# Gate and up of three feed-forward parts in seven block products instead of eight

## The chip, the cores and the metric

The kernel runs on one core of a Trainium2 chip. The metric is the device time of one execution in microseconds (us); the time given for a kernel is the median of several executions. The profile is one execution, recorded by the hardware. PE is TensorE (matmuls), PEld its weight loads, DVE is VectorE, ACT is ScalarE, POOL is GpSimd, SP issues the DMAs.

## The reference, cut to what matters

One step of an encoder of two layers on 656 tokens (528 of a prompt, 128 new rows of a sample group), width 1024. Each layer is: feed-forward, mixing (state space and latent attention in the first layer, forgetting attention and retention in the second), feed-forward. After each of the six steps comes `x = LN(ALPHA*x + f(x))`. So there are four feed-forward parts, each with 2816 hidden features:

```
hid = silu(x @ w_gate) * (x @ w_up)      # 1024 -> 2816, twice
f   = hid @ w_down                       # 2816 -> 1024
x   = LN(ALPHA * x + 0.5 * f)
```

## The kernel before, in words

Features lie on the partitions, tokens along the columns. The tokens are in two halves, h=0 with 336 and h=1 with 320 columns (320 and 320 from the last feed-forward part on). A feature dimension of 1024 is 8 tiles of 128, the hidden one 22 tiles. Every number is held as a sum of two parts of reduced precision (fp32r), a high one and a low one, so that each product is three matmuls: high by high, high by low, low by high (`mm3`, L286).

The work of a feed-forward part is a list of jobs (`ffn_part`, L406): in four groups of 5, 6, 6 and 5 hidden tiles (`PARTS`) a gate and an up job for each hidden tile, then 8 down jobs. A gate or up job has 8 input tiles: 24 matmuls for each half. A weight tile comes by DMA into a raw slot of the ring, ScalarE writes its high part into a pair slot (`hi`, L274) and VectorE the low part, raw less high (`sub`, L277). ScalarE takes silu of the gate from PSUM (L416); VectorE multiplies by up (L284); ScalarE and VectorE split the result into high and low hidden parts. `dense` (L353) runs each job for h=0, and for h=1 a few jobs later.

At the end of a part each half has its layer norm (`layer_norm`, L508, `scaled`, L541): the mean by two matmuls from column sums (that of h=1 is the "mean" of the second half below), on VectorE the differences and the sum of the squares (ending in the "fold", tile `ffn_lnva`), the variance by one more matmul, a Newton step for the root (tiles `ffn_sg`), products with it into `ffn_lnt`, and from there the next x: high part on ScalarE (L563), x itself on GpSimd (L564, tile `keep_y`), low part on VectorE (L277, tile `keep_x`). While the second half has its layer norm, PE runs the first jobs of what comes next on h=0. Six pair slots let it go six jobs, 144 matmuls, ahead.

The order within each engine is set before the run, by a scheduler with its own estimate of durations; each engine takes its list in that order and waits by semaphores. Where a wait is given by hand (`behind`, the tables `LN_SUBS` and `LN_AFTER`), an instruction is put behind a named step of the layer norm.

## Time and profile before

| | |
|---|---|
| executions | 2788.96, 2790.32, 2798.34 us |
| median | 2790.32 us |
| span of the profiled execution, first to last instruction | 2785.8 us |
| mean granted clock of TensorE | 0.974 |
| PE, DVE, ACT, POOL busy | 2696.4, 1195.6, 851.6, 452.3 us |
| stages of the span | feed-forward 1 to about 480, mixing to 870, feed-forward 2 to 1340, feed-forward 3 to 1840, mixing to 2290, feed-forward 4 to 2764, last layer norm to 2786 |

The table is read from the page, the times and the stretches of the timeline. The span leaves out what lies before the first and after the last instruction. "Granted clock" is the share of TensorE's full 2.4 GHz. Busy time of PE counts a pipelined stream of matmuls as one, so the rate is read as a stretch divided by its number of matmuls.

### The profile page before, as it was taken

To read this page: it belongs to the slowest core of one execution; us is meant where nothing else is said; L and a number is where in the kernel's file an instruction comes from. 1 tells how busy PE (TensorE), PEld (TensorE's weight loads), DVE (VectorE), ACT (ScalarE), POOL (GpSimd) and SP (SyncE) were. 2 spreads that over 40 slices of the span, in tenths; PEclk is the share of its full clock that TensorE was granted. 3 is DMA by queue.
4 is the path that set the end of the run, shared out by engine and by line. 5 is a ranking of instruction groups with operands and counts; after the bars stand their busy time and mean duration, and the time that the engine had idled before them with its cause. 6 is when DMAs were issued, how large, how long until landed. Compare 5 with 4: busy or idle time off the path is not lost.

```text
span 2785.8 us, 42647 instructions
## 1 busy us (share of the span) xinstructions
PE 2696.4 (97%) x17840; PEld 2547.3 (91%) x17840; DVE 1195.6 (43%) x2094; ACT 851.6 (31%) x1509; POOL 452.3 (16%) x569
## 2 busy tenths in 40 slices
PE   9999999899999999999999999989999999999997
PEld 8999999887678999999899999968868889999996
DVE  7343333654347333333733333365332585333335
ACT  3222222435434222222422222243343343222222
POOL 1233311651115000000500000052110041000002
PEclk9999999978999999999999999989999999999998
DMA  4323222342212222222222222112145242222221
GB/s 153 93 90 107 94 92 72 115 123 76 67 50 76 69 80 73 73 80 59 71 68 80 72 71 80 59 55 85 46 159 172 59 140 64 88 67 83 71 70 53
DMA packets 97987, 233.61 MB, mean 84 GB/s; under 512 B 14321, under 2 KB 32898, under 8 KB 97794
## 3 DMA queue, kind: packets, MB, share of 16 engines
q1 hardware_dynamic: 91266, 209.57, 24.6%
q0 software_dynamic: 6528, 21.30, 2.5%
q8 instruction: 140, 2.29, 0.3%
q14 instruction: 53, 0.43, 0.0%
...
## 4 chain that ended last, share of the span: by engine, by line
PE 89%; DVE 5%; POOL 2%; ACT 2%; issue 2%; DMA 1%; DVEq 0%; ACTq 0%; POOLq 0%; SPq 0%
PE psum L255 87%; PE psum L258 2%; POOL keep_y L564 2%; DVE ffn_lnva L284 1%; DVE ffn_sg L284 1%; DVE keep_y L284 1%; DVE ring_pair L277 1%; DVE keep_x L277 1%; DVE ffn_lnt L284 1%; ACT ring_pair L274 0%; DMA ring_raw<-oout 0%; DMA s_w<-d_w 0%; DVE ffn_sg L574 0%; DVE ffn_sg L573 0%; ACT ffn_sg L571 0%
## 5 line engine op out<-in xcount | busy, mean ns | idle before, releaser
L255 PE MATMUL psum<-keep_x,ring_pair 128*128 128x320 f32 (+2 forms) x10608 | 1675.4, 316 | 42.6 <-ACT keep_x L563 13.3
L255 PEld LDWEIGHTS psum<-keep_x,ring_pair 128*128 128x128 f32 (+1 forms) x10608 | 1609.4, 190 | 80.8 <-DVE keep_x L277 24.0
L255 PE MATMUL psum<-ffn_hid,ring_pair 128*128 128x320 f32 (+1 forms) x4224 | 653.8, 312 | 0.0
L255 PEld LDWEIGHTS psum<-ffn_hid,ring_pair 128*128 128x128 f32 x4224 | 635.3, 188 | 1.8 <-issue 0.4
L277 DVE TENSOR_TENSOR ring_pair<-ring_raw,ring_pair 128x1024 fp32r<-128x1024 f32 (+3 forms) x341 | 380.3, 1116 | 554.6 <-ACT ring_pair L274 548.7
L274 ACT ACTIVATE ring_pair<-ring_raw 128x1024 fp32r<-128x1024 f32 (+3 forms) x361 | 343.0, 953 | 868.4 <-PE psum L255 818.3
L284 DVE TENSOR_TENSOR keep_y<-keep_y,psum 128x320 f32<-128x320 f32 (+3 forms) x256 | 139.2, 555 | 282.8 <-PE psum L255 282.5
L284 POOL TENSOR_TENSOR ffn_acc<-keep_y 128x320 f32<-128x320 f32 (+1 forms) x12 | 11.7, 979 | 1390.7 <-DVE keep_y L284 1341.7
L274 ACT ACTIVATE ffn_hid<-ffn_sg 128x320 fp32r<-128x320 f32 (+1 forms) x176 | 83.2, 473 | 321.3 <-DVE ffn_sg L284 321.2
L284 DVE TENSOR_TENSOR ffn_sg<-psum,ffn_sg 128x320 f32<-128x320 f32 (+1 forms) x176 | 87.1, 495 | 214.1 <-PE psum L255 214.0
L416 ACT ACTIVATE ffn_sg<-psum 128x320 f32<-128x320 f32 (+1 forms) x176 | 77.1, 439 | 218.9 <-PE psum L255 218.8
L277 DVE TENSOR_TENSOR ffn_hid<-ffn_sg,ffn_hid 128x320 fp32r<-128x320 f32 (+1 forms) x176 | 101.2, 575 | 66.4 <-ACT ffn_hid L274 66.4
L564 POOL TENSOR_SCALAR keep_y<-ffn_lnt,keep_cst 128x320 f32<-128x320 f32 (+1 forms) x80 | 89.2, 1127 | 65.1 <-DVE ffn_lnt L284 65.1
L284 POOL TENSOR_TENSOR ffn_acc<-ffn_acc,keep_y 128x320 f32<-128x320 f32 (+1 forms) x60 | 62.3, 1039 | 114.9 <-DVE keep_y L284 100.0
L429 DVE SCALAR_TENSOR_TENSOR keep_y<-keep_y,psum 128x336 f32<-128x336 f32 (+1 forms) x64 | 31.6, 494 | 90.0 <-PE psum L255 89.8
L277 DVE TENSOR_TENSOR keep_x<-keep_y,keep_x 128x320 fp32r<-128x320 f32 (+3 forms) x89 | 59.9, 685 | 22.4 <-POOL keep_y L564 16.6
L563 ACT ACTIVATE keep_x<-ffn_lnt,keep_cst 128x320 fp32r<-128x320 f32 (+1 forms) x80 | 47.3, 650 | 51.9 <-DVE ffn_lnt L284 51.9
L916 POOL TENSOR_SCALAR even_prompt_prob<-even_prompt_prob,even_prompt_sm 80x80 f32<-80x80 f32 (+5 forms) x48 | 27.6, 576 | 145.0 <-DVE even_prompt_sm L915 132.5
L255 PE MATMUL psum<-keep_x,even_gate_pair 128*128 128x336 f32 (+1 forms) x288 | 49.6, 321 | 1.1 <-ACT even_prompt_k L1113 0.7
L277 POOL TENSOR_TENSOR ring_pair<-ring_raw,ring_pair 128x1024 fp32r<-128x1024 f32 (+1 forms) x20 | 48.5, 2425 | 5.3 <-PE psum L255 5.2
L255 PEld LDWEIGHTS psum<-keep_x,even_gate_pair 128*128 128x128 f32 x288 | 43.3, 188 | 2.9 <-ACT even_prompt_k L1113 0.9
L913 DVE TENSOR_REDUCE even_prompt_nmx<-psum 80x1 f32<-80x80 f32 (+5 forms) x48 | 25.2, 526 | 33.5 <-PE psum L255 33.2
...
## 6 DMA issues: line engine op xcount, KB each, us to landing
...
```

Source lines behind the costliest of these rows:

```text
L255: return self.nc.tensor.matmul(out, lhsT, rhs, start=start, stop=stop)
L258: self.nc.tensor.transpose(out, in_, ident)
L274: return self.nc.scalar.activation(out, in_, AF.Copy, scale=scale)
L277: return (eng or self.nc.vector).tensor_tensor(out, a, b_r.bitcast(F32), ALU.subtract)
L284: return (eng or self.nc.vector).tensor_tensor(out, a, b, op)
L416: nc.scalar.activation(sg, ps[:, :n], AF.Silu)
L429: nc.vector.scalar_tensor_tensor(y[:, m], y[:, m], 2 * ALPHA, ps[:, :n], ALU.mult, ALU.add)
L563: at["xh", h, m] = nc.scalar.activation(xh[:, m], tm, AF.Identity, scale=g[:, m:m + 1], bias=b[:, m:m + 1])
L564: at["y", h, m] = nc.gpsimd.tensor_scalar(y[:, m], tm, g[:, m:m + 1], b[:, m:m + 1], ALU.mult, ALU.add)
L913: nc.vector.reduce_max(nmx[:rows], sc[:rows, :cols], axis=AX.X, negate=True)
L916: nc.gpsimd.tensor_scalar(p[:rows, :cols], p[:rows, :cols], sm[:rows], 1.0, ALU.mult, ALU.mult)
```

## The change

Gate and up of feed-forward parts 2, 3 and 4 (`bffn`) are computed in blocks. Two hidden tiles (a pair), two halves of the input features (4 tiles each) and two equal halves of the tokens (328 columns, in the last part 320) make a 2 by 2 by 2 product. Before it is 8 block products of 12 matmuls. The change forms sums of weight blocks and sums of x blocks and does with 7 products, P1 to P7, each added into a PSUM bank in a chain: X takes P1, P6, P7, P4, and is copied away between them (`snap`); Y takes P5 and P3; W takes P2.

- Weights: two raw tiles for each pair, gate and up apart. VectorE forms four sums of [128, 512], and each of seven blocks is split into high and low (`bform`) into half a pair slot.
- x: the four sums (`combos`) are formed and split after the second half's layer norm, before each of the three parts. For the input tiles that only sums read (m < 4 of h=1) the layer norm writes x alone, on ScalarE.
- Start of a part: the six gate and up jobs of the first three pairs run their (first hidden tile, first token half) quadrant the ordinary way, 24 matmuls each (`bjob_a`), and load their weights a second time later for the five products that are left.
- The last two products of a job run between the first two of the next one (`run`).
- Groups of hidden tiles are 6, 6, 6, 4 (`SPARTS`). In the last group all eight down jobs run for h=0, then all eight for h=1.
- The ring for these parts has 4 raw and 4 pair slots (8 half slots), before 3 raw and 6 pair slots. The hidden tiles, x sums and tables of the mixing steps share memory anew.

```diff
+    def combos(self):
+        V, w = self.nc.vector, self.wid
+        y = self.Y3
+        b11, b12, b21, b22 = (y[:, 4 * i:4 * i + 4, self.cols(j)] for i in range(2) for j in range(2))
+        at, bt = self.ab("A", F32R), self.ab("B", F32R)
+        def form(tl, c):
+            v = tl[:, 2624 * c:2624 * c + 8 * w].rearrange("p (i k n) -> p i k n", i=2, k=4)
+            return v[:, 0], v[:, 1]
+        xb = lambda i, j: tuple(x[:, 4 * i:4 * i + 4, self.cols(j)] for x in self.X3)
+        f = self.forms_x = dict(P1=xb(0, 0), P2=xb(1, 0), P3=xb(1, 1), P5=xb(0, 1), P6=form(at, 0), P7=form(at, 1), P4=form(bt, 0))
+        for c in (0, 2):
+            s = slice(c, c + 2)
+            def tmp(tag):
+                return self.t(tag, [128, 2, 336], F32, 2, self.lnr)[:, :, :w]
+            def out(p, d):
+                self.split(d, f[p][0][:, s], f[p][1][:, s])
+            d1 = tmp("lnt")
+            self.tt(d1, b11[:, s], b12[:, s], ALU.subtract)
+            d2 = tmp("lnt")
+            V.scalar_tensor_tensor(d2, d1, -1.0, b22[:, s], ALU.mult, ALU.subtract)
+            out("P6", d2)
+            out("P5", d1)
+            d3 = tmp("lnsq")
+            self.tt(d3, b22[:, s], b12[:, s], ALU.subtract)
+            out("P7", d3)
+            d4 = tmp("lnsq")
+            V.scalar_tensor_tensor(d4, d2, -1.0, b21[:, s], ALU.mult, ALU.subtract)
+            out("P4", d4)
+    def bmm(self, ps, f, p, start):
+        xh, xl = self.forms_x[p]
+        for i in range(4):
+            for n, (a, x) in enumerate(((f[:, 0, i], xh[:, i]), (f[:, 0, i], xl[:, i]), (f[:, 1, i], xh[:, i]))):
+                self.nc.tensor.matmul(ps, a, x, start=start and i + n == 0, stop=i == 3 and n == 2, skip_group_check=not start)
+    def bform(self, src):
+        f = self.forms[0]
+        self.forms.rotate(-1)
+        self.split(src, f[:, 0], f[:, 1])
+        return f
...
+    def bconsume(self, gu, q, fi, bank, add, sign):
+        nc = self.nc
+        r, c = q
+        if gu == 0:
+            if q == (0, 0) and add is None:
+                g = self.t("sg", [128, 336], F32, 2, self.fr[0])[:, :self.wid]
+            else:
+                if r == c and (q == (0, 0) or fi not in self.gt):
+                    self.gt[fi] = self.t("lnsq", [128, 2, 336], F32, 2, self.lnr)
+                if q == (1, 0):
+                    self.gt[fi] = self.t("lnsq", [128, 2, 336], F32, 2, self.lnr)
+                g = self.gt[fi][:, c if r == c else r, :self.wid]
+            if add is None:
+                nc.scalar.activation(g, bank, AF.Silu, scale=float(sign))
+            else:
+                self.tt(g, bank, add, ALU.add)
+                nc.scalar.activation(g, g, AF.Silu, scale=float(sign))
+            self.g[fi, q] = g
+            return
+        g = self.g.pop((fi, q))
+        src = bank
+        if add is not None:
+            self.tt(add, bank, add, ALU.add)
+            src = add
+        if sign > 0:
+            self.tt(g, src, g, ALU.mult)
+        else:
+            nc.vector.scalar_tensor_tensor(g, src, -1.0, g, ALU.mult, ALU.mult)
+        hh, hl = (x[:, fi + r, self.cols(c)] for x in self.hidt)
+        self.split(g, hh, hl)
+    def bjob_a(self, ff, p, gu, i):
+        w = self.job_fetch(self.job(self.I["wgu"][ff, 2 * p, gu], None, None), i, LN_AFTER, LN_POOL)
+        ps = self.ps("mm")[:, :self.wid]
+        self.bmm(ps, w[:, :, 0:4], "P1", True)
+        s1 = self.t("s1", [128, 336], F32, 6, self.strr)[:, :self.wid]
+        self.nc.scalar.copy(s1, ps)
+        self.bmm(ps, w[:, :, 4:8], "P2", False)
+        self.pairs.append(w)
+        self.bconsume(gu, (0, 0), 2 * p, ps, None, 1)
+        return s1
+    def bjob(self, ff, p, gu, f0, s1=None):
+        nc, V, w = self.nc, self.nc.vector, self.wid
+        fi = 2 * p - f0
+        raws = []
+        for k in range(2):
+            raw = self.raw[0]
+            self.raw.rotate(-1)
+            self.dma(raw, self.I["wgu"][ff, 2 * p + k, gu])
+            raws.append(raw)
+        a11, a12, a21, a22 = (r[:, 4 * i:4 * i + 4] for r in raws for i in range(2))
+        lead = s1 is not None
+        X = self.ps("mm")[:, :w]
+        def snap(add):
+            u = self.ut[:, len(us), :w]
+            us.append(u)
+            if add is None:
+                nc.scalar.copy(u, X)
+            else:
+                self.tt(u, X, add, ALU.add)
+            return u
+        us = []
+        if not lead:
+            f = self.bform(a11)
+            self.bmm(X, f, "P1", True)
+            s1 = self.t("s1", [128, 336], F32, 6, self.strr)[:, :w]
+            nc.scalar.copy(s1, X)
+            yield
+            f = self.bform(a12)
+            W = self.ps("mm")[:, :w]
+            self.bmm(W, f, "P2", True)
+            self.bconsume(gu, (0, 0), fi, W, s1, 1)
+            yield
+        ut = self.ut = self.t("lnt", [128, 2, 336], F32, 2, self.lnr)
+        s3 = self.t("ws", [128, 4, 128], F32, 2, self.hidr)
+        self.tt(s3, a11, a21, ALU.add)
+        self.tt(a21, a21, a22, ALU.add)
+        self.tt(a11, a21, a11, ALU.add)
+        f = self.bform(a11)
+        self.bmm(X, f, "P6", lead)
+        self.ut = ut
+        u2 = snap(s1 if lead else None)
+        yield
+        f = self.bform(a21)
+        Y = self.ps("mm")[:, :w]
+        self.bmm(Y, f, "P5", True)
+        yield
+        f = self.bform(s3)
+        self.bmm(X, f, "P7", False)
+        self.ut = ut
+        u3 = snap(s1 if lead else None)
+        self.bconsume(gu, (1, 1), fi, Y, u3, -1)
+        yield
+        f = self.bform(a22)
+        self.bmm(X, f, "P4", False)
+        self.bconsume(gu, (1, 0), fi, X, s1 if lead else None, -1)
+        yield
+        self.tt(a12, a11, a12, ALU.add)
+        f = self.bform(a12)
+        self.bmm(Y, f, "P3", False)
+        self.bconsume(gu, (0, 1), fi, Y, u2, 1)
+        yield
+    def bffn(self, ff, ln_idx, last=False, blocks=False):
+        nc = self.nc
+        self.g, self.gt = {}, {}
+        nparts = len(SPARTS)
+        s1 = {}
+        f0, f1 = SPARTS[0]
+        n = 0
+        for p in range(f0 // 2, f1 // 2):
+            for gu in range(2):
+                s1[p, gu] = self.bjob_a(ff, p, gu, n)
+                n += 1
+        self.forms = deque(x[:, :, k:k + 4] for x in self.pairs for k in (0, 4))
+        waiting = None
...
+        def run(job, full):
+            nonlocal waiting
+            steps = 5 if full else 3
+            for i in range(steps):
+                next(job)
+                if i < 2:
+                    advance(waiting)
+            if waiting is not None:
+                assert next(waiting, 0) == 0
+            waiting = job
...
+        ahead = None
+        for pi, (f0, f1) in enumerate(SPARTS):
+            todo = [(p, gu) for p in range(f0 // 2, f1 // 2) for gu in range(2)]
+            for p, gu in todo:
+                if ahead is not None:
+                    ahead = None
+                    continue
+                run(self.bjob(ff, p, gu, f0, s1.get((p, gu))), (p, gu) not in s1)
+            if pi < nparts - 1:
+                p2 = f1 // 2
+                ahead = self.bjob(ff, p2, 0, f1)
+                run(ahead, True)
+                jobs = [down(pi, m) for m in range(8)]
+                for m, j in enumerate(jobs):
+                    wt = self.job_load(j)
+                    for h in range(2):
+                        self.job_run(j, h, wt)
+                        if m == 0:
+                            advance(waiting)
+                    self.pairs.append(wt)
+                assert next(waiting, 0) == 0
+                waiting = None
+        pi = nparts - 1
+        jobs = [down(pi, m) for m in range(8)]
+        halves = deque(x[:, :, k:k + 4] for x in self.pairs for k in (0, 4))
...
+        self.layer_norm(0, ln_idx, 4.0, last, blocks)
+        for m, j in enumerate(jobs):
+            with self.behind(*[("mean", 0, 0)] * (m >= LN_FREE), *[("var", 0, 0)] * (m >= 8 - LN_VAR)):
+                self.job_run(j, 1, w[m])
+        self.layer_norm(1, ln_idx, 4.0, last, blocks)
+        self.pairs = full
...
+            if blocks and h == 1:
+                self.combos()
...
+            elif blocks and m < 4:
+                at["y", h, m] = nc.scalar.activation(y[:, m], tm, AF.Identity, scale=g[:, m:m + 1], bias=b[:, m:m + 1])
...
-        self.ring_more("right", 2, 2)
+        self.ring_more("right", 3, 0)
...
-        self.ring_more("right", 1, 3)
+        self.ring_more("right", 2, 1)
...
-            self.ffn(1, 2)
-            self.ffn(2, 3)
+            self.bffn(1, 2, blocks=True)
+            self.bffn(2, 3)
...
-            self.ffn(3, 5, last=True)
+            self.bffn(3, 5, last=True)
```

Two places in the order of the engines, both at the entry of feed-forward part 3. First PE, before: from the last jobs on the first half (336 columns) past the variance matmul (`ffn_lnva`) of the second half to the first matmuls that read the second half (320 columns).

```order
L255 MATMUL psum<-keep_x_66,ring_pair_6826 128x336 x22
L255 MATMUL psum<-keep_x_66,ring_pair_6827 128x336 x2
L255 MATMUL psum<-ffn_lnva_6841,keep_cst_65 128x320
L255 MATMUL psum<-keep_x_66,ring_pair_6827 128x336 x22
L255 MATMUL psum<-keep_x_66,ring_pair_6828 128x336 x24
L255 MATMUL psum<-keep_x_66,ring_pair_7194 128x320
L255 MATMUL psum<-keep_x_66,ring_pair_7195 128x320
L255 MATMUL psum<-keep_x_66,ring_pair_6825 128x320
L255 MATMUL psum<-keep_x_66,ring_pair_7194 128x320 x3
```

And PE after; `ring_pair` holds weights, `abA` one of the x sums, and `keep_x` with 328 columns is x or the x sum of P5.

```order
L267 MATMUL psum<-ffn_lnva_6844,keep_cst_65 128x320
L549 MATMUL psum<-keep_x_66,ring_pair_6830 128x328
L549 MATMUL psum<-keep_x_66,ring_pair_6831 128x328 x12
L549 MATMUL psum<-keep_x_66,ring_pair_6832 128x328 x12
L549 MATMUL psum<-keep_x_66,ring_pair_6833 128x328 x12
L549 MATMUL psum<-keep_x_66,ring_pair_6832 128x328 x12
L549 MATMUL psum<-keep_x_66,ring_pair_6833 128x328 x12
L549 MATMUL psum<-keep_x_66,ring_pair_6830 128x328
L549 MATMUL psum<-keep_x_66,ring_pair_6832 128x328
L549 MATMUL psum<-keep_x_66,ring_pair_6830 128x328 x5
L549 MATMUL psum<-keep_x_66,ring_pair_6832 128x328 x5
L549 MATMUL psum<-abA_11135,ring_pair_6830 128x328
```

The last row of each is the first that reads the second half. In both, PE has 144 matmuls on the first half before it needs the second; before, the next one reads `keep_x` of h=1 as the layer norm writes it, after, it reads sums formed from it.

Then DVE, before: from the fold of the second half's layer norm on.

```order
L284 TENSOR_TENSOR ffn_lnva_6841<-ffn_lnva_6841 128x320
L277 TENSOR_TENSOR ring_pair_6827<-ring_raw_7193,ring_pair_6827 128x1024
L284 TENSOR_TENSOR ffn_sg_6835<-psum,ffn_sg_6835 128x336
L277 TENSOR_TENSOR ffn_hid_6833<-ffn_sg_6835,ffn_hid_6833 128x336
L284 TENSOR_TENSOR ffn_sg_6834<-psum,ffn_sg_6834 128x336
L277 TENSOR_TENSOR ffn_hid_6833<-ffn_sg_6834,ffn_hid_6833 128x336
L284 TENSOR_TENSOR ffn_sg_6846<-ffn_sg_6847 128x320
L573 SCALAR_TENSOR_TENSOR ffn_sg_6846<-psum,ffn_sg_6846 128x320
L574 TENSOR_SCALAR ffn_sg_6846<-ffn_sg_6846 128x320
L284 TENSOR_TENSOR ffn_sg_6847<-ffn_sg_6847,ffn_sg_6846 128x320
L284 TENSOR_TENSOR ffn_lnt_6838<-keep_y_64,ffn_sg_6847 128x2x320
L284 TENSOR_TENSOR ffn_lnt_6837<-keep_y_64,ffn_sg_6847 128x2x320
```

And DVE after, the last part of the 53 rows from the fold (which stands there as before) to the last x sum that P6 takes; `ring_raw` and `hid_ws` with 512 columns are sums of weight blocks.

```order
L289 TENSOR_TENSOR keep_x_66<-ffn_lnt_6841,keep_x_66 128x2x328
L289 TENSOR_TENSOR abA_11135<-ffn_lnsq_6843,abA_11135 128x656
L540 SCALAR_TENSOR_TENSOR ffn_lnsq_6842<-ffn_lnt_6840,keep_y_64 128x2x328
L296 TENSOR_TENSOR ffn_lnt_6841<-keep_y_64 128x2x328
L289 TENSOR_TENSOR abA_11135<-ffn_lnt_6840,abA_11135 128x656
L296 TENSOR_TENSOR ffn_lnsq_6843<-keep_y_64 128x2x328
L289 TENSOR_TENSOR abB_11136<-ffn_lnsq_6842,abB_11136 128x656
L533 SCALAR_TENSOR_TENSOR ffn_lnt_6840<-ffn_lnt_6841,keep_y_64 128x2x328
L289 TENSOR_TENSOR keep_x_66<-ffn_lnt_6841,keep_x_66 128x2x328
L289 TENSOR_TENSOR abA_11135<-ffn_lnsq_6843,abA_11135 128x656
L540 SCALAR_TENSOR_TENSOR ffn_lnsq_6842<-ffn_lnt_6840,keep_y_64 128x2x328
L289 TENSOR_TENSOR abA_11135<-ffn_lnt_6840,abA_11135 128x656
```

Between the fold and these rows stand 20 instructions of 512 columns that form and split weight blocks. The low parts of x (`keep_x<-keep_y`) stay for four tiles, and 15 instructions of 656 columns, sums of x and their low parts, are added up to the last row.

## Rows read from the trace of the kernel before

**Rows 1.** The page: engines' busy time, then the chain by engine.
```profile
PE 2696.4 (97%) x17840; PEld 2547.3 (91%) x17840; DVE 1195.6 (43%) x2094; ACT 851.6 (31%) x1509; POOL 452.3 (16%) x569
...
PE 89%; DVE 5%; POOL 2%; ACT 2%; issue 2%; DMA 1%; DVEq 0%; ACTq 0%; POOLq 0%; SPq 0%
```
**Rows 2.** Stretches of the span: columns in the first line, instructions in brackets.
```profile
core 0: us, PE busy (x) PEld busy (x) DVE busy (x) ACT busy (x) POOL busy (x), PEclk, DMA share, GB/s
...
910.00:1340.00 430.00, 430.00 (x2863) 430.00 (x2863) 139.83 (x206) 98.46 (x148) 5.90 (x7) 1.00 0.24 73
1340.00:1400.00 60.00, 55.28 (x331) 50.98 (x330) 47.11 (x67) 33.89 (x48) 35.03 (x26) 0.97 0.21 68
...
2310.00:2740.00 430.00, 430.00 (x2934) 430.00 (x2933) 147.98 (x224) 107.12 (x164) 12.33 (x12) 1.00 0.24 72
```
**Rows 3.** Groups by shape on DVE: busy us, mean ns | idle before, releaser.
```profile
L277 DVE TENSOR_TENSOR ring_pair<-ring_raw,ring_pair 128x1024 fp32r<-128x1024 f32 x205 | 255.9, 1249 | 304.6 <-ACT ring_pair L274 300.6 <-DMA fox_sample_fvc<-fvn 3.2 <-DMA fox_sample_fkc<-fkt 0.5
...
L284 DVE TENSOR_TENSOR ffn_sg<-psum,ffn_sg 128x320 f32<-128x320 f32 x110 | 53.7, 488 | 104.9 <-PE psum L255 104.8
...
L284 DVE TENSOR_TENSOR ffn_lnt<-keep_y,ffn_sg 128x640 f32<-128x640 f32 x28 | 22.6, 832 | 0.2
...
L277 DVE TENSOR_TENSOR ring_pair<-ring_raw,ring_pair 128x512 fp32r<-128x512 f32 x8 | 5.4, 692 | 7.1 <-ACT ring_pair L274 7.0
...
L284 DVE TENSOR_TENSOR retention_kx<-retention_kt,odd_oc 128x512 f32<-128x512 f32 x4 | 2.7, 684 | 0.0
```
**Rows 4.** Groups by shape on ACT.
```profile
L416 ACT ACTIVATE ffn_sg<-psum 128x320 f32<-128x320 f32 x110 | 47.4, 431 | 68.7 <-PE psum L255 68.7
...
L274 ACT ACTIVATE ring_pair<-ring_raw 128x512 fp32r<-128x512 f32 x8 | 4.9, 630 | 8.9 <-DMA ring_raw<-ewout 8.9
```
**Rows 5.** Timeline of PE, entry of feed-forward 3: start, us, what [idle before].
```profile
1354.18 0.83 PE L255 MATMUL psum<-ffn_lnva,keep_cst 128*128 128x336 f32 x2 [1.21 <-DVE ffn_lnva L284]
...
1358.36 0.81 PE L255 MATMUL psum<-ffn_acc,keep_cst 128*128 128x320 f32 x2 [1.14 <-POOL ffn_acc L284]
...
1360.96 1.01 PE L255 MATMUL psum<-keep_x,ring_pair 128*128 128x336 f32 x3 [1.20 <-ACT keep_x L563]
...
1386.91 6.54 PE L255 MATMUL psum<-keep_x,ring_pair 128*128 128x320 f32 x38 [0.37 <-DVE keep_x L277]
```
**Rows 6.** Timeline of DVE, the same place.
```profile
1358.41 0.48 DVE L284 TENSOR_TENSOR keep_y<-keep_y,psum 128x320 f32<-128x320 f32 x1
1358.81 0.50 DVE L284 TENSOR_TENSOR ffn_sg<-ffn_sg,ffn_sg 128x336 f32<-128x336 f32 x1
...
1369.69 3.27 DVE L277 TENSOR_TENSOR keep_x<-keep_y,keep_x 128x336 fp32r<-128x336 f32 x2
...
1376.32 0.49 DVE L284 TENSOR_TENSOR ffn_lnva<-ffn_lnva 128x320 f32<-128x320 f32 x1
```
**Rows 7.** Timeline of POOL, the same place.
```profile
1369.95 2.64 POOL L277 TENSOR_TENSOR ring_pair<-ring_raw,ring_pair 128x1024 fp32r<-128x1024 f32 x1
```
**Rows 8.** Stretches of PE around an idle time: busy (matmuls), granted clock, DMA.
```profile
866.00:870.00 4.00, 0.62 (x5) 0.96 0.45 133
870.00:874.00 4.00, 3.46 (x8) 0.50 0.44 131
874.00:878.00 4.00, 4.00 (x20) 0.68 0.00 0
878.00:882.00 4.00, 4.00 (x28) 1.00 0.31 68
```
**Rows 9.** Timeline of PE, entry of feed-forward 4.
```profile
2294.43 0.81 PE L255 MATMUL psum<-ffn_acc,keep_cst 128*128 128x320 f32 x2 [0.52 <-POOL ffn_acc L284]
...
2298.89 6.88 PE L255 MATMUL psum<-keep_x,ring_pair 128*128 128x320 f32 x45 [1.52 <-DVE keep_x L277]
2306.19 2.28 PE L255 MATMUL psum<-keep_x,ring_pair 128*128 128x320 f32 x14 [0.42 <-DVE ffn_sg L284]
```
**Rows 10.** Timeline of DVE, the same place.
```profile
2306.81 0.49 DVE L284 TENSOR_TENSOR ffn_lnva<-ffn_lnva 128x320 f32<-128x320 f32 x1
```

More of the change, by code (lines that the diff above doesn't have):

```diff
@@ L242, in t, with put, ab @@
         return v
+    def put(self, reg, tag, tiles):
+        reg["tags"][tag] = (tiles, [0])
+    def ab(self, tag, dt):
+        w = dict(A=5984, B=2624)[tag]
+        self.abn += 1
+        return self.abr["pool"].tile([128, w], dt, name=f"ab{tag}{self.abn}", tag=tag)
     def ps(self, tag, cols=512):
@@ L538, in layer_norm, with scaled @@
         else:
-            self.scaled(h, idx, last, rs)
-    def scaled(self, h, idx, last, rs):
+            self.scaled(h, idx, last, rs, blocks and h == 1)
+            if blocks and h == 1:
+                self.combos()
+    def scaled(self, h, idx, last, rs, blocks=False):
         nc = self.nc
@@ L1319, in even_mix @@
         self.ffn_open(1, "right", False)
+        self.str_open("right")
+        self.hid_open("right")
         ks = (slice(0, 4), slice(4, 8))
```

151 lines of the change are left out of this document (108 added, 43 removed).

## The prediction

> **What bounds the kernel now.** I read the page first: PE is busy for 2696.4 of the 2785.8 us of the span, and 89% of the chain that ended last lies on PE, 5% on DVE [rows 1]. So what PE has to do and what it waits for set the time. Then the stretches: inside a feed-forward part PE has no idle time at 430 us on end, and 2863 matmuls in 430 us make 150.2 ns for one (146.6 ns in part 4, where both halves have 320 columns); DVE and ACT are busy for 140 to 148 and 98 to 107 us of them [rows 2]. Then the shapes of DVE and ACT for prices [rows 3, 4], and last the timelines where one part passes into the next, since there PE waits for a layer norm: 55.28 us busy of 60 at the entry of part 3 [rows 2].
>
> **What is removed.** A part has 44 gate and up jobs of 48 matmuls, 2112. After, 22 jobs (a pair of hidden tiles, gate or up) of 84 make 1848: 264 fewer, 792 in three parts. At the rates above (264 x 2 x 150.2 ns + 264 x 146.6 ns) that is 118.0 us of PE time. The mean number of columns is as before, and so I take the rate as unchanged.
>
> **What is added in the steady stretch.** Per job seven blocks of [128, 512] are split, not two tiles of [128, 1024], and four sums formed. On DVE a low part is 692 ns and a sum 684 ns (the nearest row with both inputs in SBUF), an operation of 320 columns 488 ns [rows 3]. A gate job: 7 x 0.69 + 4 x 0.68 + 3 additions x 0.49 = 9.0 us. An up job has 8 more of 0.49, four products and four low parts: 13.0 us. A pair costs DVE 22.0 us; PE needs 2 x 84 x 0.150 = 25.2 us for it. ACT: 7 x 0.63 + 7 x 0.43 = 7.4 us in each job [rows 4], 14.8 in the pair. So an up job alone costs DVE more than PE's 12.6 us, but eight half slots let it run eight blocks, 14 us, ahead, and gate and up alternate. PE stays the bound, with cover of 3 us in 25. If DVE needed 10% more it would become the bound, and each further us per pair would cost 8 pairs x 3 parts = 24 us.
>
> PSUM: bank X is copied away between products, P6, copy, P7, copy, P4: two places in a job, 132 in all. In the order one other product, 12 matmuls or 1.8 us, always stands between. A copy takes 0.43 us and may stand behind a high part of 0.63 us [rows 4], 1.06 us together, so the product covers it. From nothing to 1.06 us each this is 0 to 140 us; I take 0.06 us, by the cover, 8 us for all small waits of this kind. The 18 more weight loads of 512 KB lie under a DMA share of 0.24 [rows 2], at no cost; without that cover one is 7 us at the 73 GB/s of that stretch [rows 2], 129 us in all.
>
> **What is added at the three entries.** This is the large term. T is the mean of the second half, 1358.36 at the entry of part 3. PE begins there on the first half at T + 2.6, after its last wait of 1.20, and comes to the second half at T + 28.5, when that is just ready (waits of 0.37 us and less) [rows 5]. After, the 144 matmuls on the first half end about T + 2.6 + 144 x 0.150 = T + 24. What PE needs next is not x but P5 and P6's sums, on DVE behind the whole layer norm.
>
> DVE ends the fold at T + 18.4 (1376.81) [rows 6]; one low part of a weight tile lies in this time that after stands behind it, so T + 17. From there to the last sum that P6 takes stand 53 rows, 55 instructions: 20 of 512 columns (13.8 us), 15 of 656 (at the 0.83 of 640: 12.5), 4 of 640 (3.3), 13 of 320 or 328 (6.4), 2 of 1024 (2.5) and one short: 38.8 us. Where instructions do not need each other they start 0.08 us closer (1358.41 to 1358.81 for one of 0.48) [rows 6]: 34.4 us at the least. So P6 is complete between T + 51.4 and T + 56; I take T + 54, near the long end, as many of the 55 need the one before. By then PE has done the 144 and at most 36 more, of the 504 that it has until the six led jobs are through. 324 are left: 324 x 0.150 = 48.6, end at T + 102.6. Without any wait it would be T + 2.6 + 504 x 0.150 = T + 78.2. DVE is no later bound: all its 119 instructions to the end of the led jobs make 68 to 78 us, from T + 17 to T + 95 at most. The loss is 24.4 us. To that comes the clock: after 3.9 us without work PE was granted 0.50 for 4 us and 0.68 for the next 4, then 1.00 again [rows 8], which loses 2.0 + 1.3 us; of this I count 2.5, since some falls where PE waits anyway. About 1 us of waits that are there today go away. An entry costs 26 us; parts 2 and 3 have the same list: 52 us.
>
> Part 4: T is 2294.43 [rows 9], the fold ends at T + 12.9 [rows 10]. Seven instructions of 512 columns come before the fold (4.5 us), one of 1024 goes: T + 16. From there 41 instructions, 25 to 29 us by the same prices, to P6: T + 43. Here 38 of the 144 matmuls stand ahead of T, so 466 are left from T on, 68.3 us at 146.6 ns; after P6 324 x 0.1466 = 47.5, end at T + 90.5. Loss 22.2, clock 2.5, today's waits of 1.52 and 0.42 [rows 9] gone: 23 us.
>
> POOL bears on this. While it ran an instruction of 2.64 us [rows 7], two low parts of x on DVE took 3.27 us, not twice 0.49 [rows 6]: 2.3 us more. The Trainium skill says in "SBUF — State Buffer", section "Who interferes with whom", that GpSimd and a VectorE instruction with two SBUF inputs exclude each other for whole instructions; the trace agrees. By that rule alone the four steps that POOL keeps in the second half's norm could hold the sums up by some 4 us more at an entry, and the forecast would be 12 us later; this is inside the range below.
>
> **What is gained at the ends of parts.** For the first half's norm PE had five jobs of 15 matmuls as cover and waited 1.21, 1.14 and 1.20 us [rows 5]. After, eight jobs of 12 are 21 matmuls more, 3.1 us. That is worth 3 us at the end of part 2 and 1 at that of part 3; at the end of part 4 the chain after the last matmul is the same. I take 4 us.
>
> **The sum.** -118.0 + 75 (entries) + 8 (small waits) - 4 (ends) = -39 us on the profiled execution. The span is 2785.8, and the median of the runs 2790.3, 4.5 us more for what lies around it; I subtract from the median: 2751, forecast 2750 us. Bounds: entries of 20 us (back to back, no clock loss) to 32 us (waits among the engines, the full clock loss twice), 60 to 95 in all, and small waits of 0 to 20: 2725 to 2785 us as this case's own range.
>
> **Rivals.**
> The sums are hidden: DVE's list at the entry runs as fast as PE leads, as DVE's 43% busy [rows 1] would have it. Against it: 47.1 of 60 us are busy at an entry already [rows 2]. With only 3 us lost at each it gives 2790 - 118 - 4 + 9 + 3 = 2680 us.
>
> The copies out of X take the place of the matmuls saved. ACT and DVE take their lists in order, a copy stands behind whatever waits there, and PE stands at P7 or P4 until it is done; 132 places. It decides from 0.30 us each on (39 us / 132), and at 0.5 us each it gives 2750 - 8 + 66 = 2808 us, slower than before. For it: 0.43 + 0.63 us of work can stand before each release [rows 4]. Against it: the 1.8 us between.
>
> VectorE sets the pace in the pairs: at 15% over the prices, 25.3 us a pair, with waits for ACT on top, 1.5 us lost per pair for 24 pairs, 2750 + 36 = 2786 us.
>
> The clock falls in the block stretches too, by short gaps between products: two restarts of 2.5 us in each of 22 x 3 jobs would be 330 us, one in every fourth job 41 us, 2790 us. Against it: gaps of 1.21, 1.14 and 1.20 us within 7 us are there today, and the stretch around them reads 0.97 [rows 2, 5]. The Trainium skill tells of such a case in "TensorE: Matmul & The Clock Gate", section "A second HAM failure mode: psum-queue depth-cycling": rotating through PSUM banks left small gaps and the clock swung between its two levels. No run here shows it yet in a steady stretch.
>
> **How the numbers follow.** Chances: forecast 0.62, sums hidden 0.12, copies 0.13, VectorE's pace 0.08, clock 0.05. What can be told from no change here is about 0.3%, 8 us. Faster, under 2782: the forecast less 0.04 at its upper end, the hidden sums, 0.02 of the mild cases: 0.72. Within: 0.04 of the forecast, half of pace and clock, a little of the copies: 0.12. Slower: 0.16. Range for 8 in 10: 2690, towards the hidden sums, to 2805, to mild copies.
>
> **What would show it.** PE should have 792 matmuls less; its idle time should stand in three blocks of 15 to 25 us, each released by DVE (`keep_x` or `ab`), about 24 us after the second half's mean, with a granted clock near 0.5 right after. In stretches of full jobs PE should be busy throughout at about 150 ns a matmul and clock 1.00, with DVE at three quarters. I am wrong if the waits at `ab` are under 8 us each, if PE waits at the starts of P7 and P4 for the copy, or if DVE is over 95% busy in the full jobs.

## The result, and the profile after

The changed kernel takes 2771.3 us (median of 4 runs, 2767.4 to 2772.9) against 2790.8 of the kernel before: ratio 0.9916, 95% interval 0.9898 to 0.9934. The forecast was 2750. The sign is right, and the time lies in the range, but only 19.5 us came of 40. The page, engines and chain, answers to [rows 1]:
```profile
PE 2627.8 (95%) x17048; PEld 2461.8 (89%) x17048; DVE 1607.6 (58%) x2940; ACT 1064.4 (38%) x2010; POOL 440.4 (16%) x557
...
PE 88%; DVE 6%; ACT 2%; issue 2%; DMA 1%; POOL 1%; SPq 0%; DVEq 0%; ACTq 0%; POOLq 0%
```
PE has the 792 matmuls less (17840 to 17048), but is busy only 68.6 us less. To see where the rest went I cut both traces at the second half's mean of each layer norm. First the kernel before: first mixing step, parts 2 and 3, second mixing step, part 4.
```profile
498.15:870.54 372.39, 349.12 (x2057) 284.96 (x2057) 183.44 (x402) 148.70 (x334) 119.95 (x210) 0.90 0.30 87
870.54:1358.36 487.82, 484.59 (x3181) 480.45 (x3181) 185.73 (x271) 131.21 (x194) 40.99 (x32) 0.99 0.24 72
1358.36:1844.06 485.70, 483.34 (x3180) 479.56 (x3181) 183.88 (x273) 128.66 (x193) 32.96 (x29) 1.00 0.23 68
1844.06:2294.43 450.37, 420.92 (x2915) 350.93 (x2913) 229.02 (x424) 180.75 (x386) 100.47 (x139) 0.95 0.34 109
2294.43:2762.65 468.22, 466.28 (x3165) 464.58 (x3166) 175.40 (x262) 121.48 (x182) 24.45 (x23) 1.00 0.23 68
```
The same five stretches of the changed kernel, and below them three from the middle of its parts (the second holds gate and up jobs alone):
```profile
core 0: us, PE busy (x) PEld busy (x) DVE busy (x) ACT busy (x) POOL busy (x), PEclk, DMA share, GB/s
498.21:880.84 382.63, 360.53 (x2057) 292.30 (x2057) 185.32 (x402) 145.91 (x332) 116.03 (x210) 0.86 0.29 86
880.84:1352.17 471.33, 449.84 (x2916) 444.21 (x2916) 325.06 (x555) 200.01 (x360) 37.19 (x28) 0.97 0.27 82
1352.17:1821.04 468.87, 449.37 (x2917) 444.64 (x2918) 318.11 (x552) 198.31 (x358) 31.90 (x30) 0.97 0.25 76
1821.04:2303.26 482.22, 444.06 (x2936) 366.70 (x2935) 233.24 (x428) 188.79 (x394) 103.44 (x136) 0.91 0.31 101
2303.26:2748.23 444.97, 431.70 (x2880) 427.12 (x2879) 305.98 (x539) 190.60 (x346) 18.58 (x17) 0.98 0.25 78
960.00:1290.00 330.00, 330.00 (x2198) 329.85 (x2197) 208.52 (x368) 131.65 (x245) 0.00 (x0) 1.00 0.27 82
1040.00:1111.00 71.00, 71.00 (x474) 71.00 (x474) 51.45 (x94) 37.35 (x75) 0.00 (x0) 1.00 0.25 77
2400.00:2700.00 300.00, 300.00 (x2047) 300.00 (x2046) 187.67 (x331) 119.83 (x223) 0.00 (x0) 1.00 0.27 82
```
The parts became 16.5, 16.8 and 23.3 us shorter, 56.6 in all, more than the whole forecast. The mixing steps, which compute what they did before, became 10.2 and 31.9 us longer. Of the 31.9, 3.1 are 21 matmuls of part 4 that now stand ahead of its mean (2936 against 2915, at 146.6 ns): the second step itself lost 28.8. Against the forecast's sum:

| term | forecast | measured |
|---|---|---|
| 792 matmuls, rate unchanged | -118.0 | -118.0 |
| entries, ends, small waits | +79 | +64.5 (118.0 - 56.6 + 3.1) |
| first mixing step | no term | +10.2 |
| second mixing step | no term | +28.8 |
| before and after these | no term | -0.2 |
| span | -39 | -14.7 |

The medians differ by 5 us more than the spans. In the changed kernel the profiled run is 1.6 us above its median, and 1.8 us lie around its span (2772.9 against 2771.1). In every run on record it is 1.7 to 2.0 us; of the 4.5 that the forecast took for the kernel before, the rest is a profiled run below its median.

The entry of part 3 on PE, which answers to [rows 5]; T is 1352.17:
```profile
1352.17 0.81 PE L267 MATMUL psum<-str_s,keep_cst 128*128 128x320 f32 x2 [3.42 <-POOL str_s L296]
...
1377.94 3.85 PE L549 MATMUL psum<-keep_x,ring_pair 128*128 128x328 f32 x24 [0.97 <-ACT str_s L597]
1394.56 0.92 PE L549 MATMUL psum<-keep_x,ring_pair 128*128 128x328 f32 x2 [12.77 <-ACT keep_x L286]
1397.69 3.10 PE L549 MATMUL psum<-keep_x,ring_pair 128*128 128x328 f32 x10 [2.22 <-DVE keep_x L289]
1400.60 2.38 PE L549 MATMUL psum<-abA,ring_pair 128*128 128x328 f32 x12
...
1405.97 7.29 PE L549 MATMUL psum<-abA,ring_pair 128*128 128x328 f32 x46 [0.19 <-DVE abA L289]
```
The led products end at T + 29.6, PE waits 12.8 us for the first sum of x (P5's, formed in `keep_x`), and from T + 53.8 it runs on without a wait. The four waits make 15.6 us. DVE meanwhile, which answers to [rows 6]:
```profile
1369.06 1.22 DVE L289 TENSOR_TENSOR ring_pair<-ring_raw,ring_pair 128x1024 fp32r<-128x1024 f32 x1
...
1375.15 0.48 DVE L296 TENSOR_TENSOR ffn_sg<-ffn_sg 128x320 f32<-128x320 f32 x1
...
1385.44 1.56 DVE L296 TENSOR_TENSOR ffn_lnt<-keep_y,ffn_sg 128x640 f32<-128x640 f32 x2
...
1392.56 1.17 DVE L296 TENSOR_TENSOR ffn_lnt<-keep_y 128x656 f32<-128x656 f32 x1
...
1405.08 0.83 DVE L289 TENSOR_TENSOR abA<-ffn_lnt,abA 128x656 fp32r<-128x656 f32 x1
```
The fold ends at T + 17, as forecast, and the first low part of led weights follows at 1369.06, the first step of the square root comes at 1375.15, the normalisation only at 1385.44, the first sum of x at 1392.56. Between them stand sums and low parts of weights.

In the second mixing step the sample group's stage stands out:
```profile
2052.01 0.66 PE L270 MATMUL psum<-keep_cst,fox_sample_prob 128*128 128x128 f32 x4 [1.42 <-ACT fox_sample_prob L2048]
...
2079.28 0.66 PE L270 MATMUL psum<-keep_cst,fox_sample_prob 128*128 128x128 f32 x4 [1.25 <-ACT fox_sample_prob L2048]
...
2081.74 1.84 PE L267 MATMUL psum<-fox_sample_fkc,abA 128*32 128x512 f32 x5
2083.51 0.33 PE L270 MATMUL psum<-keep_cst,abA 128*128 128x128 f32 x1
2083.59 3.17 PE L267 MATMUL psum<-keep_x,ring_pair 128*128 128x336 f32 x19
```
From 2029 on PE has the sample group alone and waits at softmax after softmax; the first input product of retention (`keep_x`, `ring_pair`) comes at 2083.59, right behind the last product on a cached key (`fox_sample_fkc`). In the kernel before such products ran between the steps, as here:
```profile
2057.61 3.03 PE L255 MATMUL psum<-keep_x,ring_pair 128*128 128x320 f32 x19
2060.48 0.60 PE L258 MATMUL psum<-keep_cst,fox_sample_prob 128*128 128x128 f32 x4
```
The new layout suggests why: the first buffer of `fkc` is columns 0 to 511 of the region that also holds `rx`, the temporary of the rotation that each query and key product of retention needs, and the sample group is written ahead of retention.

### The profile page after: what moved, and what is told of

It is laid out like the page before. It is cut to its first block, busy times and chain, and to the rows that moved or that the text cites. A ratio compares the mean times of both kernels' runs of the same rounds, so it can differ in the third digit from the quotient of the medians.

```text
span 2771.1 us, 42830 instructions
## 1 busy us (share of the span) xinstructions
PE 2627.8 (95%) x17048; PEld 2461.8 (89%) x17048; DVE 1607.6 (58%) x2940; ACT 1064.4 (38%) x2010; POOL 440.4 (16%) x557
## 3 DMA queue, kind: packets, MB, share of 16 engines
q1 hardware_dynamic: 93858, 219.01, 25.2%
## 4 chain that ended last, share of the span: by engine, by line
PE 88%; DVE 6%; ACT 2%; issue 2%; DMA 1%; POOL 1%; SPq 0%; DVEq 0%; ACTq 0%; POOLq 0%
PE psum L267 58%; PE psum L549 27%; PE psum L270 2%; DVE ffn_lnt L296 1%; POOL keep_y L869 1%; DVE ffn_lnva L296 1%; DVE ffn_sg L296 1%; DVE keep_x L289 1%; DVE ring_pair L289 1%; ACT ring_pair L286 1%; DVE keep_y L296 0%; DMA even_in_raw<-uv 0%; DVE ring_raw L296 0%; DVE abA L289 0%; DMA ring_raw<-wdn 0%
## 5 line engine op out<-in xcount | busy, mean ns | idle before, releaser
L286 ACT ACTIVATE ring_pair<-ring_raw 128x512 fp32r<-128x512 f32 (+3 forms) x607 | 448.7, 742 | 824.6 <-PE psum L267 498.6
L267 PE MATMUL psum<-keep_x,ring_pair 128*128 128x320 f32 (+2 forms) x4272 | 700.6, 322 | 31.1 <-ACT ring_pair L286 7.6
L267 PEld LDWEIGHTS psum<-keep_x,ring_pair 128*128 128x128 f32 (+1 forms) x4272 | 657.6, 192 | 54.8 <-DVE keep_x L289 13.0
L289 DVE TENSOR_TENSOR ring_pair<-ring_raw,ring_pair 128x512 fp32r<-128x512 f32 (+3 forms) x587 | 485.1, 829 | 333.7 <-ACT ring_pair L286 321.8
L267 PE MATMUL psum<-hid_hid,ring_pair 128*128 128x320 f32 (+1 forms) x4224 | 650.5, 313 | 2.9 <-DVE ffn_lnt L296 2.3
L267 PEld LDWEIGHTS psum<-hid_hid,ring_pair 128*128 128x128 f32 x4224 | 636.2, 188 | 6.3 <-ACT ring_pair L286 3.4
L549 PE MATMUL psum<-keep_x,ring_pair 128*128 128x328 f32 (+1 forms) x3168 | 526.1, 318 | 46.0 <-ACT keep_x L286 25.9
L549 PEld LDWEIGHTS psum<-keep_x,ring_pair 128*128 128x128 f32 x3168 | 493.3, 193 | 55.0 <-ACT keep_x L286 26.7
L549 PE MATMUL psum<-abA,ring_pair 128*128 128x328 f32 (+1 forms) x1584 | 262.0, 313 | 1.2 <-ACT abA L286 0.7
L549 PEld LDWEIGHTS psum<-abA,ring_pair 128*128 128x128 f32 x1584 | 243.7, 190 | 2.8 <-DVE abA L289 1.3
L296 POOL TENSOR_TENSOR str_s<-keep_y 128x320 f32<-128x320 f32 (+1 forms) x12 | 13.3, 1110 | 1033.9 <-DVE keep_y L296 950.9
```

The lines of the kernel that those rows point to most:

```text
L267: return self.nc.tensor.matmul(out, lhsT, rhs, start=start, stop=stop)
L286: return self.nc.scalar.activation(out, in_, AF.Copy, scale=scale)
L289: return (eng or self.nc.vector).tensor_tensor(out, a, b_r.bitcast(F32), ALU.subtract)
L296: return (eng or self.nc.vector).tensor_tensor(out, a, b, op)
L549: self.nc.tensor.matmul(ps, a, x, start=start and i + n == 0, stop=i == 3 and n == 2, skip_group_check=not start)
```

## The experiments

Lengths are from the traces, mean to mean. The parts of the changed kernel are 471.3, 468.9 and 445.0 us, its mixing steps 382.6 and 482.2.

**e1. The key buffer elsewhere.**
```diff
-self.put(post, "fkc", [oa[:, 0:512]] + [self.t(f"fkc{i}", [128, 512]) for i in range(3)])
+self.put(post, "fkc", [oar(512)] + [self.t(f"fkc{i}", [128, 512]) for i in range(3)])
 self.put(post, "pn", [oar(256)])
-self.put(post, "on", [oar(128) for _ in range(2)])
```


> The changed kernel, with one piece of its memory put elsewhere: the first of the four buffers for cached keys in the second mixing step no longer lies over the temporaries that the rotation of queries and keys uses (`rx`), but in the free end of the same region; the two output buffers `on` get memory of their own. Theory A (this overlap is most of what the second mixing step lost): the input products of retention can run between the steps of the sample group again, since their rotation need not wait for the last cached key; PE stands in the sample stage no more, its clock stays at 1.00 there (27 us at 0.50 today), and the step, mean to mean, goes from 482.2 us to 455 to 462 (450.4 in the kernel before); whole program 2744 to 2751 us against 2771. Rival B (the loss comes from other memory, such as the ring with fewer slots for pairs, or from the retention stage itself): the step stays at 478 to 485 us, the program at 2766 to 2773.

2747.3 us, ratio 0.9843 (0.9823 to 0.9863); once more as e9 2744.2 (0.9825, 0.9799 to 0.9851). PE in the sample stage, and the whole step below:
```profile
2025.42 0.49 PE L267 MATMUL psum<-fox_sample_fbr,fox_sample_fbl 128*128 128x512 f32 x2
...
2027.48 3.04 PE L267 MATMUL psum<-keep_x,ring_pair 128*128 128x320 f32 x19
2030.36 0.60 PE L270 MATMUL psum<-keep_cst,fox_sample_prob 128*128 128x128 f32 x4
```
```profile
1812.48:2275.54 463.06, 432.84 (x2936) 361.64 (x2935) 233.64 (x428) 182.47 (x389) 103.40 (x136) 0.93 0.32 105
```
The products stand between the steps again, PE waits for no softmax there, and the step is 463.1 us (460.8 in e9): 19 to 21 of the 28.8 us were this one overlap. Theory A holds, one us above its range. The edit also moves `on`; that was not tested apart, but its old place, the free end, is not shared with `rx`. The spans of the two traces differ by 28 us, and 10 of these lie in the first mixing step, which the edit does not touch: so part of e1's gain is luck. Of the 7 to 10 us left in the second step (3 to 6 against the second trace of the kernel before, e10), about 3 lie between the two means of the step's last norm (41.4 us against 34.8, of which 3.1 are the moved matmuls), where PE stands 4.0 us for an addition of VectorE; this was not tested.

**e2. The first mixing step's layout.**
```diff
+self.hid_open("left", False)
+self.str_open("left", False)
 self.ffn_open(1, "left", True)
 self.ffn_open(0, "left", False)
-self.str_open("left", False)
-self.hid_open("left", False)
```


> The changed kernel, with the regions of the first feed-forward part opened in another order: the hidden features lie at the bottom again, as in the kernel before, and the layer norm's temporaries above them, so that the first mixing step's tiles `lat`, `wq` and `tk` lie over memory that is free before the layer norm of the second half. Theory A (those tiles wait for the layer norm's temporaries, the instructions are put in another order, and PE later has nothing large to run beside the small S5 products): the first mixing step, mean to mean, goes from 382.6 us to 371 to 376 (372.4 in the kernel before), with about 75 us of it at clock 0.50 instead of 102; the whole program 2759 to 2764 us. Rival B (the 10 us come from elsewhere, such as the wait for the output projection's first weights, 6.05 us, or the shared tile of the sample group): the step stays at 380 to 384 us, the program at 2767 to 2773.

2768.5 us (0.9921, 0.9907 to 0.9936). The first step took 386.0 us: no gain, A falls; Rival B's range is missed too, by 2 us. The later repeats say more. The instructions up to the end of this step are the same, in the same order on every engine, in the changed kernel and in e1, e4, e5 and e6, and the step took 382.6, 373.0, 380.2, 374.8 and 381.7 us. In e8 and e11, with the same list up to there, it took 376.8 and 378.5.

**e7, e9, e10. The same kernels again.**

> The changed kernel as it is, once more. Theory A (the first mixing step's 382.6 us are no cost of the change: e1, with the same instructions in the same order up to there, took 373.0, e4 380.2, and the time lies at clock 0.50 in 102, 78 and 92 us of it): another execution gives another length between 372 and 383 us, with 10 us more of it for each 20 us more at clock 0.50, while the second step stays at 478 to 485 us and the parts within 1 us. Rival B (the length belongs to the program): 382 to 383 us again.

> The kernel of e1 once more. Theory A (the first mixing step's length is drawn anew in each execution, between 372 and 384 us, with the time that the clock spends at 0.50): anything from 372 to 384 us, the second step again 461 to 465 us. Rival B (it belongs to the program as built): 373.0 us again within 1 us.

> The kernel before once more. Theory A (as in e9): a first mixing step between 372 and 384 us where it was 372.4. Rival B: 372.4 again within 1 us.

First step of the changed kernel, e1 and the kernel before, each from its second trace:
```profile
497.97:881.08 383.11, 359.10 (x2056) 290.44 (x2056) 185.23 (x402) 145.93 (x332) 116.11 (x210) 0.88 0.29 86
```
```profile
498.28:873.61 375.33, 353.43 (x2057) 287.12 (x2057) 185.01 (x402) 146.05 (x332) 116.07 (x210) 0.89 0.29 88
```
```profile
499.80:873.07 373.27, 349.30 (x2056) 285.21 (x2056) 184.01 (x402) 148.12 (x334) 119.51 (x210) 0.90 0.30 87
```
Rival B holds in e7 and e10, and e9 is 2.3 us off it: in two traces each kernel nearly repeats its own length. Two are few: the four executions of e1 lie between 2741.6 and 2754.3 us, and no trace shows where they differ. Still, e1 and the changed kernel differ by 7 to 10 us here with the same instructions in the same order. What goes with the length is the clock: TensorE stood at 0.50 for 104 and 96 us of the step in the changed kernel, for 80 and 86 in e1, 76 and 76 before. PE's idle time in the step did not grow from before to after (23.3 and 22.1 us); its busy time did, by 11.4 us, with the same 2057 matmuls. So the 10.2 us are time at the lower clock. As e1 has the same list and the same place of the hidden features and took 373.0, neither is enough to explain them. What tips the clock stays open. The second step took 482.0 us in e7 and 454.3 in e10, 3.9 more than in the first trace of the kernel before: its loss is known as 25 to 29 us.

**e3 and e11. The entries: sums left out.** In e3 `combos` forms nothing and the products take parts of x. In e11, on e1, the led jobs form no weight sums:
```diff
-f = self.forms_x = dict(..., P5=xb(0, 1), P6=form(at, 0), P7=form(at, 1), P4=form(bt, 0))
+f = self.forms_x = dict(..., P5=xb(0, 1), P6=xb(0, 0), P7=xb(0, 1), P4=xb(1, 0))
```
```diff
+if lead:
+    s3 = a21
+else:
     self.tt(s3, a11, a21, ALU.add)
...
-self.tt(a12, a11, a12, ALU.add)
+if not lead:
+    self.tt(a12, a11, a12, ALU.add)
```


> The changed kernel without the sums of x at the three entries: P5, P6, P7 and P4 take parts of x as they stand, so what is computed is not the reference's; the weight sums and all else stay. Theory A (the forecast's large term: at the entries PE waits for the sums of x on VectorE behind the layer norm): the three parts, 471.3, 468.9 and 445.0 us from mean to mean, come down by 15 to 24 us each, towards the 448, 446 and 430 that the old lengths less 264 matmuls make; the whole program 2705 to 2725 us. Rival B (the forecast's large term is not the sums but what else VectorE has in its queue there, weight sums and low parts of weights ahead of the norm): 3 to 10 us each, 2740 to 2762 us. Rival C (the parts lose in the steady stretches or at their ends): no part changes by over 3 us, 2762 to 2773 us.

> The kernel of e1 without the weight sums of the led jobs: P6, P5, P7 and P3 take blocks as they stand there, so what is computed is not the reference's; the low parts of the weights and the sums of x stay. VectorE's list gets shorter by 24 instructions of 0.68 us per entry, about 15 us, none of which is a sum of x. Theory A (any work of VectorE up to the end of the led jobs counts, as e3, e5 and e8 leave it): each part 8 to 15 us shorter than e1's 471.5, 468.9 and 444.9 us, as with the sums of x left out; the whole program 2705 to 2723 us against 2744 to 2747. Rival B (only the chain norm, sums of x, P6 counts): 0 to 5 us each, 2730 to 2747 us.

e3: 2726.8 us (0.9772, 0.9756 to 0.9789), just above A's range; e11: 2726.6 us (0.9758, 0.9730 to 0.9786). Their parts 2, 3 and 4, one fence each:
```profile
872.55:1329.73 457.18, 446.39 (x2917) 442.18 (x2917) 312.84 (x539) 194.47 (x352) 37.06 (x28) 0.99 0.27 85
1329.73:1782.68 452.95, 446.21 (x2917) 442.14 (x2917) 305.63 (x536) 191.96 (x350) 30.20 (x26) 0.99 0.25 77
2262.93:2695.82 432.89, 426.76 (x2881) 422.52 (x2880) 293.86 (x523) 184.38 (x338) 16.87 (x16) 1.00 0.26 80
```
```profile
876.32:1340.32 464.00, 448.50 (x2916) 443.83 (x2917) 311.11 (x531) 200.74 (x360) 35.88 (x28) 0.98 0.27 84
1340.32:1801.33 461.01, 448.92 (x2917) 443.80 (x2917) 304.31 (x528) 197.74 (x358) 31.01 (x30) 0.98 0.25 78
2264.69:2701.67 436.98, 429.17 (x2880) 425.00 (x2879) 293.17 (x515) 190.39 (x346) 18.85 (x17) 0.99 0.25 79
```
Without the sums of x the parts lose 14.1, 15.9 and 12.1 us, one inside A's range and two 1 and 3 us under it, for 12 us of VectorE work each. Without the weight sums, 13 to 14 us of work, they lose 7.5, 7.9 and 7.9, under A's range and over B's. So work that is no part of the norm and of x counts as well, at about half its length. The traces show which half. In the changed kernel 12 of the 24 weight sums of the entry of part 3 start ahead of P6's last sum (1370.19 to 1394.40), each taking 0.60 us of the list: 7.2 us. PE's last wait of that entry, first in e1 (T at 1343.55), then the first and the last in e11 (T at 1340.32):
```profile
1397.50 7.28 PE L549 MATMUL psum<-abA,ring_pair 128*128 128x328 f32 x46 [0.17 <-DVE abA L289]
```
```profile
1376.22 0.92 PE L549 MATMUL psum<-keep_x,ring_pair 128*128 128x328 f32 x2 [5.54 <-ACT keep_x L286]
...
1386.79 1.77 PE L549 MATMUL psum<-keep_x,ring_pair 128*128 128x328 f32 x10 [0.15 <-DVE keep_x L289]
```
PE runs on from T + 46.5 instead of T + 54.0, 7.5 us earlier, and that is the gain. The 12 sums behind left nothing to be seen: it is the list ahead of the sums that counts, as the forecast had it, not the list up to the end of the led jobs.

**e4, e5, e6. Another order on VectorE.** e4 puts the sums in the order of need. e5, on e1, queues the weight work of the led jobs behind P5's sums; e6 does both.
```diff
+for c, s in sl.items():
+    self.tt(d1[c], b11[:, s], b12[:, s], ALU.subtract)
+    V.scalar_tensor_tensor(d2[c], d1[c], -1.0, b22[:, s], ALU.mult, ALU.subtract)
+    out("P6", c, d2[c])
+for c in sl:
+    out("P5", c, d1[c])
...
```
```diff
+late = [("sum", "P5", 2)] * (lead and 2 * (p - f0 // 2) + gu >= LED_FREE)
+with self.behind(*late):
     self.tt(s3, a11, a21, ALU.add)
```


> The changed kernel with the sums of x in the order in which PE needs them: both halves of P6, then P5, P7, P4, and the low parts of x for P3 last; the same instructions. Theory A (PE waits for P6's sums): they are complete after 6 of the 16 instructions instead of 11 or 13, so the last wait of each entry is 4 to 6 us earlier and each part that much shorter, 10 to 17 us in all: 2754 to 2761 us. Rival B (VectorE's whole list up to the end of the led jobs is the bound): the wait only moves to P7 or P4 or to the weight sums, the parts keep their lengths within 2 us, 2766 to 2773 us.

> The kernel of e1, and at the three entries VectorE's sums and low parts of weights of all led jobs but the first are queued behind the sums of x for P5 (the same instructions in another order; the order of the sums themselves as in the changed kernel). Theory A (the 22 us of weight work that stand ahead of the second half's normalisation hold the sums of x up; the list as a whole is not the bound): the first sum of x comes some 10 us earlier than T + 40, PE's long wait of 12.8 us falls to 5 us or less, and each part becomes 4 to 9 us shorter than e1's 471.5, 468.9 and 444.9 us; whole program 2723 to 2737 us against e1's 2747. Rival B (VectorE's whole list up to the end of the led jobs is the bound, so that what is put behind is only late later): the wait moves to the second led job's products, the parts stay within 2 us, 2742 to 2752 us.

> The kernel of e5 with the sums of x in the order of need as in e4. Theory A (with the weight work out of the way the order of the sums counts): 1 to 4 us less per part than e5, 2715 to 2733 us. Rival B (no difference to e5, as e4 made none to the changed kernel): within 4 us of e5.

e4: 2769.0 us (0.9920, 0.9905 to 0.9934), parts 471.2, 468.4, 444.5. e5: 2758.5 (0.9880, 0.9864 to 0.9895), parts 474.3, 469.9, 446.7. e6: 2752.4 (0.9856, 0.9839 to 0.9872), parts 474.4, 469.9, 443.3. In sum no order gains. e4 lies in rival B's range; e5 is slower than e1 and above rival B's, and e6 is 6 us below e5 where rival B allowed 4. PE in e4, entry of part 3, T at 1351.00:
```profile
1393.50 0.92 PE L550 MATMUL psum<-keep_x,ring_pair 128*128 128x328 f32 x2 [12.78 <-ACT keep_x L286]
1398.39 4.19 PE L550 MATMUL psum<-keep_x,ring_pair 128*128 128x328 f32 x14 [3.98 <-DVE keep_x L289]
```
e4 did not test what it was meant to. PE takes P5's sum (`keep_x`) first in both kernels, and e4 put P5's low parts behind P6's sums: the wait for P5 stays 12.8 us, and the next grows from 2.2 to 4.0. From T + 47.4 PE waits no more, but it has 36 matmuls more ahead of it than the changed kernel has at T + 53.8. PE in e5, the same entry, T at 1346.80:
```profile
1383.40 0.64 PE L551 MATMUL psum<-keep_x,ring_pair 128*128 128x328 f32 x1 [8.13 <-ACT keep_x L287]
1386.19 1.73 PE L551 MATMUL psum<-keep_x,ring_pair 128*128 128x328 f32 x5 [2.16 <-DVE keep_x L290]
1389.21 1.73 PE L551 MATMUL psum<-abA,ring_pair 128*128 128x328 f32 x5 [1.00 <-DVE abA L290]
...
1399.34 0.92 PE L551 MATMUL psum<-abA,ring_pair 128*128 128x328 f32 x2 [2.14 <-ACT ring_pair L287]
```
The long wait fell from 12.8 to 8.1 us, and five smaller ones came behind it, the last, up to T + 52.5, for weights that were put back (in e6 up to T + 53.6). So PE needs both before it runs on, sums and weights of the led jobs, and VectorE makes both in one list. Between fold and normalisation stand some 12 us of weight work, not the 22 of the expectation.

**e8. Part of the weight work on GpSimd**, on e1:
```diff
+G = nc.gpsimd if lead else None
-self.tt(s3, a11, a21, ALU.add)
+self.tt(s3, a11, a21, ALU.add, G)
```


> The kernel of e1, and in the led jobs of each part one weight sum (for P7), the low part for P4 and the sum for P3 are formed on GpSimd instead of VectorE: 18 instructions of 512 columns less per entry on VectorE, 11 to 12 us of its list. Theory A (VectorE's list up to the end of the led jobs bounds the entry, as e4 to e6 leave it): 5 to 11 us less in each part, about 471 to 463, 469 to 461, 445 to 438; whole program 2715 to 2735 us. Rival B (GpSimd and VectorE keep each other waiting where both take two inputs from SBUF, as when two low parts took 3.27 us in the kernel before, or GpSimd is too slow and is itself waited for): VectorE's instructions grow by as much as its list loses, the parts within 2 us or longer, 2742 to 2775 us.

2774.2 us (0.9932, 0.9915 to 0.9950), 27 us above e1; parts 476.7, 472.2, 454.3 in the trace, which is of its quickest run (2764.6). Groups by shape from T + 17 to T + 100 at the entry of part 3, first three of DVE, then one of POOL:
```profile
L296 DVE TENSOR_TENSOR ring_raw<-ring_raw 128x512 f32<-128x512 f32 x7 | 8.0, 1146 | 3.8 <-POOL hid_ws L296 3.8
L296 DVE TENSOR_TENSOR ffn_lnt<-psum,str_s 128x328 f32<-128x328 f32 x10 | 4.8, 490 | 1.9 <-PE psum L549 1.8
L296 DVE TENSOR_TENSOR ffn_lnt<-keep_y,ffn_sg 128x640 f32<-128x640 f32 x4 | 4.4, 1145 | 0.0
```
```profile
L296 POOL TENSOR_TENSOR ring_raw<-ring_raw 128x512 f32<-128x512 f32 x6 | 9.1, 1519 | 12.1 <-DVE ring_raw L296 12.1
```
In e1 the same three groups of DVE took 683, 494 and 818 ns. A moved instruction took 1.41 to 1.52 us on GpSimd, and of VectorE's groups with both inputs in SBUF several grew, these two on average by two thirds and two fifths, while the one with an input in PSUM did not. Over part 3 VectorE is busy for 320.4 us with 534 instructions, in e1 for 317.6 with 552: the list has lost nothing. Rival B holds. This agrees with the Trainium skill, "SBUF — State Buffer", section "Who interferes with whom": a VectorE instruction with two SBUF inputs contends with a GpSimd instruction that reads SBUF.

## Why the prediction was half right

**Matmuls removed.** Right to the matmul and the rate: 2198 in 330.00 us are 150.1 ns, 2047 in 300.00 are 146.6.

**The steady stretch.** Right. PE has no idle time at clock 1.00, and DVE is busy for 51.45 of 71 us in gate and up jobs, 72% where the signs said three quarters (the forecast's own sum, 22.0 of 25.2 us, makes 87%). So no copy out of X, no pace of VectorE and no fall of the clock was to be seen there: these three rivals fall by rows, without a run. The swinging clock of the Trainium skill ("TensorE: Matmul & The Clock Gate", section "A second HAM failure mode: psum-queue depth-cycling") did not show in these stretches.

**The entries.** The path was right. P6 was put at T + 54, and PE runs without waits from T + 53.8; the 504th matmul on weights from T on was to end at T + 102.6, and by a count in the trace it starts at T + 102.3. PE's idle time in the parts is 21.5, 19.5 and 13.3 us (3.2, 2.4, 1.9 before). That the sums are hidden falls too: to leave them out was worth 42 us (e3). The size was too high: 64.5 us for entries, ends and small waits against 79, by part 23.2, 22.8 and 18.5. The traces show three terms that were off. The run without waits that the loss was taken from was put at T + 78.2, but in the kernel before it starts at T + 83.6, with waits and 3.4 us at half clock ahead of it; so this entry cost 19 us and not 26. The ends gained nothing: at the end of part 2 PE waits 0.99 and 3.42 us in the norm, where it waited 1.21 and 1.14. And the small waits at the copies, put at 8 us, do not show in the full jobs.

"DVE is no later bound" held as built: after T + 53.8 PE waits for nothing up to the end of the led jobs. But there was little to spare: in e5 and e6 the weights that were put behind the sums hold PE up to T + 52.5 and T + 53.6. What bounds the entry is all that VectorE has to do up to there, weights and sums alike, and not the place of one sum in it.

Two of the signs failed. The waits at `ab` are under 1 us, and the forecast called itself wrong under 8: the long wait is for P5's sum, which lies in `keep_x` and comes first, so the mechanism stands and the sign named the wrong tile. And part 4 has no block of 15 us: its 13.3 us are many waits, the longest 4.0 us, for the fold.

**The sum.** This is the step that failed. It runs "-118.0 + 75 (entries) + 8 (small waits) - 4 (ends)" and has no term for the mixing steps, though the change says that memory is laid out anew and its diff, in full, puts a buffer over `rx`. The second step cost 28.8 us, of which e1 gives back 19 to 21 by moving that buffer. The first was 10.2 longer, all of it time at the lower clock, and the cause is open. That the time still lies in the range is in part luck: the forecast of the span was 24.3 us too low, and would have been 38.8 too low had the entries, ends and small waits not been set 14.5 too high.

e1 beats both kernels: 2747.3 and 2744.2 us in its two series, with no computation changed. That it falls on the forecast's 2750 is no merit of the forecast.
